# Post-norms that read their scale from PSUM and leave GpSimd out, and bias rows copied from HBM to HBM

## The chip, the cores and the metric

The kernel runs on one core of one Trainium2 chip. Its engines are TensorE (PE in the rows, with PEld for its weight loads), VectorE (DVE), ScalarE (ACT), GpSimd (POOL) and SyncE (SP, which only issues DMAs here). The metric is the device time of one execution in microseconds. Three runs of the kernel before took 3525.71, 3531.94 and 3532.26 us, so the median is 3531.94 us.

## The reference, cut to what matters

A sequence of 512 tokens of width 1024 goes through two hybrid blocks and then through a third block of another kind. All arithmetic is float32. The change touches the third block alone: two of its norms are applied to the output of a branch, before that is added to the residual stream, and its attention has a relative bias table.

```
def rms_norm_2(x, g):
    y = x * rsqrt(mean(x * x, axis=-1, keepdims=True) + 1e-6)
    return y * g

def second_block(x, ...):                     # 512 tokens x 1024
    h = rms_norm_2(x, g_pre_mix)
    z = h @ w_in
    ...                                       # dilated attention (uses rel_bias_table) and a convolution, gated into merged
    x = x + rms_norm_2(merged @ w_mix_out, g_post_mix)
    h = rms_norm_2(x, g_pre_ffn)
    x = x + rms_norm_2(swiglu(h @ w_ffn_in) @ w_ffn_out, g_post_ffn)
    return x

bias = bias_tab[rel_bucket(offset * dilation)]   # 3 groups of 8 heads; a function of query minus key
s = q k / 8 + bias
```

## The kernel before, in words

Activations lie transposed: 8 chunks (`m` or `k`) of 128 channels by 512 tokens. Each product of a weight and an activation is made of three float32r matmuls in `mm3` (L172 high by high, L173 high weight by low activation, L174 low weight by high activation), so every activation needs a high part `h` hi (ScalarE, L239) and a low part lo (VectorE, L240, which needs the high part).

All weights come as one stream of 550 units of 128 x 1024 float32 (512 KB, tensor `wst`). SP issues the load of a unit (L133) into one of 3 staging slots. `w_prep` turns a unit into its high part (ScalarE, L141) and its low part (VectorE, L142) in a ring of 5, up to `LOOK` = 3 units ahead of the one that TensorE uses. One unit holds 8 weight tiles, which is 24 matmuls. The next load into a staging slot is issued only when L142 has read it.

Stages follow one another: `gen_ffn`, `gen_mix` with `gen_side`, `gen_merge` and `gen_ffn` for each of the two layers, then `gen_mix2` with `gen_attn2`, `gen_merge2` and the last `gen_ffn`. The Tile scheduler fixes each engine's order when the program is built, by a simulated timeline and by priorities: `with self.late(-5000)` gives what stands in it an earlier place, and `keep_in_program_order` forbids the scheduler to move an instruction past others so marked. On the chip each engine then runs its list in that order.

`gen_ffn` starts with the columns (0, 1) of gate and up in four PSUM banks, chunk k after chunk k as they arrive, and goes on with column groups 2 to 12. After (0, 1) the statistics of the norm are made: `stats_a` sums the squares over partitions with four matmuls against a column of ones (L218), takes an inverse square root by 12 small VectorE operations (L223, L205 to L210), and `bcast` makes four diagonal blocks (L231) and one matmul with ones (L232) that puts the scale of each token on all partitions of a PSUM bank; ScalarE copies that bank to SBUF (L233).

`bias_rows` is called once, in the first `gen_ffn`, after column group 2. It makes for each of 3 groups a table of 8 heads by 384 positions (L1015, L1018) in 8 partitions of SBUF, and a DMA issued by GpSimd (L1019) writes each row 128 times to `dr_b` in HBM, from where the attention of the third block reads it much later with a shifted pattern.

`post` is the norm after a branch. It is used once over all tokens at the end of `gen_merge2` (the mid post below) and twice, on 256 tokens each, at the end of the last `gen_ffn` (half 0 and half 1). The branch output lies in SBUF, already multiplied by the gain. `post` makes the statistics, copies the scale to SBUF, multiplies each chunk by it (L1351) and adds it to x (L1360). In the mid post `x_done` then makes hi, lo and the squares for the next norm, whose sum GpSimd accumulates (L200). In the two halves some chunks are multiplied and added on GpSimd, and each chunk of x goes out by a DMA on SP (L1362).

Of the kernel before, what the change touches and what calls it, by code (L numbers as in the profile page):

```python
# [9 lines left out]
F32 = mybir.dt.float32  # L10
F32R = mybir.dt.float32r
I32 = mybir.dt.int32
AF = mybir.ActivationFunctionType
ALU = mybir.AluOpType
# [32 lines left out]
A_RB = A_PA + PAR  # L47
A_SM = A_RB + 512
A_X = A_SM + 336
A_Y = A_X + 4096  # L50
# [59 lines left out]
class Build:  # L110
# [113 lines left out]
        self.rsqrt(y, v, a, b)  # L224
        return y

    def bcast(self, cols, dg, ps, out):

        nc = self.nc
        for t in range(cols.shape[-1]):  # L230
            nc.vector.tensor_scalar_mul(dg[:, 128 * t:128 * t + 128], self.f(A_C + C_ID, 128), cols[:, t:t + 1])  # L231
        nc.tensor.matmul(ps, lhsT=self.f(A_C + C_ONE, 128), rhs=dg, start=True, stop=True)  # L232
        nc.scalar.activation(out, ps, AF.Copy)  # L233

    def x_done(self, m, gain):
        hi, lo = self.h(m)
# [7 lines left out]
    def gen_ffn(self, wgu, wdn, l, done, halves=None):  # L244
        nc = self.nc
        Y = A_Y
        gs = [self.f(Y + 1536 + 512 * i, 512) for i in range(2)]
        tt = [self.f(Y + 2560 + 512 * i, 512) for i in range(2)]
        rb = self.f(A_RB, 512)
        ring = tuple(range(8))  # L250

        def fs(c):
            o = R_O + (c % FSLOTS) * 1024
            return self.r(o, 512), self.r(o + 512, 512)

        def gkey(c, up, k):
            return (wgu, l, np.arange(128 * k, 128 * k + 128), np.arange(128) + 128 * c + up * DFF)

        def evac(c, pg, pu):
            i = c % 2  # L260
            nc.vector.tensor_tensor(gs[i], pg, rb, op=ALU.mult)  # L261
            nc.scalar.activation(gs[i], gs[i], AF.Silu)
            nc.vector.tensor_tensor(gs[i], pu, gs[i], op=ALU.mult)  # L263
            hi, lo = fs(c)
            self.split(hi, lo, gs[i])

        def up(cs):
            ps = {(c, up): self.bank(ring) for c in cs for up in (0, 1)}
            order = [(c, up, k) for c in cs for up in (0, 1) for k in range(8)]
            if len(cs) == 2:  # L270
                order.sort(key=lambda e: e[2])
            for c, up, k in order:
                self.mm3(ps[c, up], self.w(gkey(c, up, k)), self.h(k), k == 0, k == 7)
                yield
            if len(cs) == 2:
                pst = self.bank(ring)
                self.bcast(self.stats_a((self.acc,), pst), tt_flat, pst, rb)
            for c in cs:
                evac(c, ps[c, 0], ps[c, 1])
            if cs[0] == 2 and self.first:  # L280
                self.first = False
                self.bias_rows()

        tt_flat = self.f(Y + 2560, 512)

        def down(grp, cs):
            nk = len(cs)
            if grp == 0:
                order = [(m, j) for m in range(8) for j in range(nk)]
            else:  # L290
                order = [(m, j) for m in range(2) for j in range(nk - 1)] + [(m, nk - 1) for m in range(2)]
                order += [(m, j) for m in range(2, 6 if halves else 8) for j in range(nk)]
            ps = {}
            for m, j in order:
                if j == 0:
                    ps[m] = self.bank(ring)
                key = (wdn, l, np.arange(128) + 128 * cs[j], np.arange(128) + 128 * m)
                self.mm3(ps[m], self.w(key), fs(cs[j]), j == 0, j == nk - 1)
                yield
                if j == nk - 1:  # L300
                    done(grp, m, ps[m], tt[m % 2], rb)
            if grp == 0 or not halves:
                return

            tl = {}
            for i in range(2):
                sl = slice(256 * i, 256 * i + 256)
                for m in (6, 7):
                    ps = self.bank(ring)[:, sl]
                    for j in range(nk):  # L310
                        if i == 0:
                            tl[m, j] = self.w((wdn, l, np.arange(128) + 128 * cs[j], np.arange(128) + 128 * m))
                        self.mm3(ps, tl[m, j], [a[:, sl] for a in fs(cs[j])], j == 0, j == nk - 1)
                        yield
                    done(grp, m, ps, tt[m % 2][:, sl], rb, sl)
                halves(i)

        c0 = list(range(11))
        c1 = list(range(11, 22))
        for cs in [(0, 1)] + [(c,) for c in range(2, 13)]:  # L320
            yield from up(cs)
        yield from down(0, c0)
        for c in c1[2:]:
            yield from up((c,))
        yield from down(1, c1)
# [679 lines left out]
    def bias_rows(self):  # L1005

        nc = self.nc
        o = A_Y + 3584
        cb = self.f(o, 2304)[0:32]
        nc.scalar.dma_start(cb, self.ap["cb"])  # L1010
        tab = self.f(o + 2304, 24)[0:32]
        nc.scalar.dma_start(tab, self.ap["par"][2][0:32, 296:320])
        for g in range(3):
            ps = self.bank(tuple(range(8)))
            nc.tensor.matmul(ps[0:8, 0:384], lhsT=tab[:, 8 * g:8 * g + 8], rhs=cb[:, 384 * g:384 * g + 384],  # L1015
                             start=True, stop=True)
            t = self.f(o + 2328 + 384 * g, 384)[0:8]
            nc.vector.tensor_tensor(t, ps[0:8, 0:384], cb[0:8, 1152 + 384 * g:1536 + 384 * g], op=ALU.add)  # L1018
            nc.gpsimd.dma_start(self.dr_b[g], t[:, None, :].to_broadcast([8, 128, 384]))  # L1019

    def gen_mix2(self):
        nc = self.nc
# [312 lines left out]
        o = R_O + 8192 + 1024 * c  # L1335
        return self.r(o, 512), self.r(o + 512, 512)

    def post(self, y, next_gain, rb, ts=range(4), pool=()):

        nc = self.nc  # L1340
        ring = tuple(range(8))
        ps = self.bank(ring)
        sl = slice(128 * ts[0], 128 * ts[-1] + 128)
        c = self.stats_a((self.acc, self.sqt[1]), ps, ts=ts)
        rb = rb[:, sl]
        self.bcast(c, self.f(A_Y + 512, 512)[:, sl], ps[:, sl], rb)
        keep = self.tc.keep_in_program_order
        y = [a[:, sl] for a in y]

        def mul(m):  # L1350
            keep(eng(m).tensor_tensor(y[m], y[m], rb, op=ALU.mult))  # L1351

        def eng(m):
            return nc.gpsimd if m in pool else nc.vector
        mul(0)
        for m in range(8):
            if m < 7:
                mul(m + 1)
            x = self.x(m)[:, sl]
            keep(eng(m).tensor_tensor(x, x, y[m], op=ALU.add))  # L1360
            if next_gain is None:
                nc.sync.dma_start(self.ap["out"][:, m, sl], x)  # L1362
            else:
                self.x_done(m, next_gain)

    def gen_merge2(self, gains):
        nc = self.nc
# [28 lines left out]
        for m, k in order:  # L1396
            if k == 0:
                ps[m] = self.bank(ring)
            self.mm3(ps[m], self.w(("w_mix_out_2", 0, np.arange(128) + 128 * k, np.arange(128) + 128 * m)), self.h(k),
                     k == 0, k == 7)  # L1400
            yield
            if k == 7:
                nc.scalar.activation(y[m], ps[m], AF.Copy)
                self.sq_acc(m, y[m], self.acc, self.sqt, apart=True)
                nc.scalar.activation(y[m], y[m], AF.Copy, scale=gains[:, 56 + m:57 + m])
        self.post(y, gains[:, 64:72], self.f(A_RB, 512))

    def ffn_post(self, gain):
        nc = self.nc
        y = [self.f(A_Y + 3584 + 512 * m, 512) for m in range(8)]  # L1410

        def done(grp, m, ps, t, rb, sl=slice(0, 512)):
            ym = y[m][:, sl]
            nc.vector.tensor_tensor(ym if grp == 0 else t, ps, rb[:, sl], op=ALU.mult)
            if grp == 1:
                nc.vector.tensor_tensor(ym, ym, t, op=ALU.add)
                self.sq_acc(m, ym, self.acc[:, sl], [a[:, sl] for a in self.sqt], apart=True)
                nc.scalar.activation(ym, ym, AF.Copy, scale=gain[:, m:m + 1])

        def half(i):  # L1420
            self.post(y, None, self.f(A_Y + 1536, 512), range(2 * i, 2 * i + 2), ((1, 2, 4, 5, 7), (2, 5))[i])
        return done, half


    def run(self, upto=99, start=0):
        tc, nc, ap = self.tc, self.nc, self.ap
        with tc.tile_pool(name="sb", bufs=1) as sb, tc.tile_pool(name="hp", bufs=1) as self.hp, \
# [9 lines left out]
            self.sqt = [self.f(A_Y + 512 + 512 * i, 512) for i in range(2)]  # L1437
            self.dr_x = dr.tile([128, 4096], F32, name="dr_x")
            self.dr_b = dr.tile([3, 8, 128, 384], F32, name="dr_b")
            self.dr_c = dr.tile([8, 128, 512], F32, name="dr_c")  # L1440
            self.dr_s = dr.tile([512, 12], F32, name="dr_s")
            self.m2 = {}
# [142 lines left out]
```

## Time and profile before

| | |
|---|---|
| median of three runs | 3531.94 us (3525.71 to 3532.26) |
| the profiled execution | 3525.48 us, its span 3523.7 us |
| TensorE busy | 3423.5 us, 97% of the span |
| VectorE, ScalarE, GpSimd busy | 57%, 37%, 9% |
| mean granted clock of TensorE | 0.985 of full speed |
| HBM traffic | 357 MB, 101 GB/s on average |

The span is the time from the first to the last instruction of one profiled execution. Matmuls are pipelined, so their single durations overlap: in steady state TensorE starts 134 of them in 30 us. What is idle on an engine other than TensorE costs nothing by itself.

### The profile page before, as it was taken

What the parts mean: (1) busy time and instruction counts of PE and PEld (TensorE: products, weight loads), DVE (VectorE), ACT (ScalarE), POOL (GpSimd) and SP (SyncE); (2) the same over time, 40 slices, a digit from 0 to 9 for tenths busy, and PEclk for the clock granted to TensorE, in tenths of its full rate; (3) what the DMA queues carried; (4) which work ended last, traced back from release to release, by engine and by line L of the source; (5) the groups of instructions that cost most, each with busy time, mean ns of one, the idle gap of its engine ahead of it and who ended that gap; (6) DMA issues with size and microseconds to landing.
All of it is one profiled execution on the core that took longest, in us unless ns stands there. A gap on an engine that the chain in (4) does not pass through costs nothing.

```text
span 3523.7 us, 43236 instructions
## 1 busy us (share of the span) xinstructions
PE 3423.5 (97%) x16884; PEld 2793.6 (79%) x16884; DVE 1998.7 (57%) x3733; ACT 1316.1 (37%) x2234; POOL 320.0 (9%) x355
## 2 busy tenths in 40 slices
PE   6899999999999999999999999999999999999997
PEld 5688888776888888888887768888877777878886
DVE  4344488566544444344886666443488998554344
ACT  3222354356332233223544464322344443443232
POOL 2000100010300010001000104000111112220002
PEclk8999999999999999999999999999999999999998
DMA  6722322331322222223322314223333224522221
GB/s 149 116 99 96 120 91 87 108 115 54 132 96 96 96 96 96 96 100 116 96 89 98 112 42 149 95 97 100 108 105 92 83 79 141 183 80 98 97 96 54
DMA packets 100814, 357.05 MB, mean 101 GB/s; under 512 B 14168, under 2 KB 16984, under 8 KB 99808
## 3 DMA queue, kind: packets, MB, share of 16 engines
q1 hardware_dynamic: 81504, 290.49, 24.6%
q0 software_dynamic: 18144, 61.76, 6.9%
q8 instruction: 132, 2.16, 0.3%
q10 hardware_dynamic: 960, 2.04, 0.2%
q14 instruction: 74, 0.61, 0.1%
HBM read 320.05 MB, written 32.08 MB: 100 GB/s over the span
## 4 chain that ended last, share of the span: by engine, by line
PE 91%; DMA 3%; DVE 3%; ACT 1%; issue 1%; POOL 0%; DVEq 0%; ACTq 0%; POOLq 0%
PE pb L172 27%; PE pb L173 27%; PE pb L174 27%; DMA af<-wst 2%; PE pb L801 2%; PE pb L793 1%; PE pb L777 1%; PE pb L1193 1%; PE pb L595 1%; PE pb L737 1%; PE pb L1290 1%; PE pb L1266 1%; PE pb L756 0%; DVE af L1351 0%; DVE ar L142 0%
## 5 line engine op out<-in xcount | busy, mean ns | idle before, releaser
L141 ACT ACTIVATE ar<-af 128x1024 fp32r<-128x1024 f32 x550 | 582.7, 1060 | 1517.5 <-PE pb L173 968.2
L172 PE MATMUL pb<-h,ar 128*128 128x512 f32 x2848 | 1114.2, 394 | 33.9 <-ACT ar L141 15.1
L174 PE MATMUL pb<-h,ar 128*128 128x512 f32 x2848 | 1120.1, 393 | 0.1
L173 PE MATMUL pb<-h,ar 128*128 128x512 f32 x2848 | 1119.4, 393 | 0.0
L142 DVE TENSOR_TENSOR ar<-af,ar 128x1024 fp32r<-128x1024 f32 x550 | 687.7, 1251 | 447.6 <-ACT ar L141 446.1
L172 PEld LDWEIGHTS pb<-h,ar 128*128 128x128 f32 x2848 | 538.0, 189 | 151.1 <-ACT h L239 16.2
L174 PEld LDWEIGHTS pb<-h,ar 128*128 128x128 f32 x2848 | 537.7, 189 | 114.6 <-issue 3.2
L173 PEld LDWEIGHTS pb<-h,ar 128*128 128x128 f32 x2848 | 537.9, 189 | 113.6 <-issue 3.2
L173 PE MATMUL pb<-ar 128*128 128x512 f32 (+1 forms) x1254 | 483.2, 386 | 1.2 <-DVE ar L183 1.2
L174 PE MATMUL pb<-ar 128*128 128x512 f32 (+1 forms) x1254 | 482.8, 386 | 0.0
L172 PE MATMUL pb<-ar 128*128 128x512 f32 (+1 forms) x1254 | 481.8, 386 | 0.6 <-DVE af L779 0.5
L172 PEld LDWEIGHTS pb<-ar 128*128 128x128 f32 x1254 | 235.6, 188 | 49.4 <-DVE af L779 1.2
L200 POOL TENSOR_TENSOR af<-af 128x512 f32<-128x512 f32 (+1 forms) x76 | 109.7, 1444 | 1816.5 <-ACT af L198 1805.5
L173 PEld LDWEIGHTS pb<-ar 128*128 128x128 f32 x1254 | 235.6, 188 | 49.0 <-DVE ar L183 2.4
L174 PEld LDWEIGHTS pb<-ar 128*128 128x128 f32 x1254 | 235.6, 188 | 47.1
L263 DVE TENSOR_TENSOR af<-pb,af 128x512 f32<-128x512 f32 x110 | 75.6, 690 | 299.0 <-PE pb L174 297.9
L261 DVE TENSOR_TENSOR af<-pb,af 128x512 f32<-128x512 f32 x110 | 75.5, 691 | 247.0 <-PE pb L174 231.9
L1132 DVE SCALAR_TENSOR_TENSOR af<-af 128x512 f32<-128x512 f32 x240 | 179.4, 748 | 3.6
L172 PE MATMUL pb<-ar,h 128*128 128x256 f32 (+1 forms) x448 | 133.4, 298 | 0.0
L173 PE MATMUL pb<-ar,h 128*128 128x256 f32 (+1 forms) x448 | 132.4, 296 | 0.0
L174 PE MATMUL pb<-ar,h 128*128 128x256 f32 (+1 forms) x448 | 132.0, 295 | 0.0
L180 DVE TENSOR_TENSOR ar<-af,ar 128x512 fp32r<-128x512 f32 (+4 forms) x178 | 114.3, 649 | 16.2 <-ACT ar L179 15.6
(236 smaller groups left out, 3185.3 us busy)
## 6 DMA issues: line engine op xcount, KB each, us to landing
af<-wst SPq DMA_DIRECT2D x550, 512.0 KB, 3.3
dr_g<-af POOLq DMA_DIRECT2D x64, 256.0 KB, 2.3
af<-dr_g POOLq DMA_DIRECT2D x24, 512.0 KB, 4.6
dr_x<-af POOLq DMA_DIRECT2D x3, 2048.0 KB, 7.5
af<-dr_x POOLq DMA_DIRECT2D x3, 2048.0 KB, 8.7
dr_b<-af POOLq DMA_DIRECT2D x3, 1536.0 KB, 63.3
h<-dr_g POOLq DMA_DIRECT2D x16, 256.0 KB, 5.5
af<-x POOLq DMA_DIRECT2D x8, 256.0 KB, 12.3
```

The lines of the kernel that those rows point to most:

```text
L141: self.nc.scalar.activation(self.r(o, UNIT), st, AF.Copy)
L142: self.nc.vector.tensor_tensor(self.r(o + UNIT, UNIT), st, self.r(o, UNIT), op=ALU.subtract)
L172: mm(out, lhsT=w[0], rhs=a[0], start=start, stop=False, skip_group_check=True)
L173: mm(out, lhsT=w[0], rhs=a[1], start=False, stop=False, skip_group_check=True)
L174: mm(out, lhsT=w[1], rhs=a[0], start=False, stop=stop, skip_group_check=True)
L180: self.nc.vector.tensor_tensor(lo, src, hi, op=ALU.subtract)
L200: nc.gpsimd.tensor_tensor(acc, acc, t, op=ALU.add)
L261: nc.vector.tensor_tensor(gs[i], pg, rb, op=ALU.mult)
L263: nc.vector.tensor_tensor(gs[i], pu, gs[i], op=ALU.mult)
L595: self.nc.tensor.transpose(ps[:, 128 * i:128 * i + 128], t[:, 128 * i:128 * i + 128], self.f(A_C + C_ID, 128))
L801: first[u] = self.behind(first[u], mm(out[64 * u:64 * u + 64], lhsT=v[u][:, j, :], rhs=pts[u][:, 128 * j:128 * j + 128], start=first[u] is ...
L1132: nc.vector.scalar_tensor_tensor(a, u[:, j:j + 512], w[:, j:j + 1], a, op0=ALU.mult, op1=ALU.add)
```

## The change

It has four parts. First, `bias_rows` is called after column group 8 instead of 2, and each table row is first written once to a new HBM tensor `dr_r` and from there copied 128 times to `dr_b` by a DMA from HBM to HBM. Second, `post` no longer copies the scale from PSUM to SBUF: VectorE's multiplication reads it from the PSUM bank. Third, `post` uses no GpSimd and no forced order, its statistics get an earlier priority, and in the two halves at the end one operation (and one DMA) takes two chunks of 128 x 256. Fourth, `gen_merge2` squares and scales straight from PSUM instead of from a copy in SBUF.

```
-    def bcast(self, cols, dg, ps, out):
+    def bcast(self, cols, dg, ps, out=None):
...
-        nc.scalar.activation(out, ps, AF.Copy)
+        if out is not None:
+            nc.scalar.activation(out, ps, AF.Copy)
...
-            if cs[0] == 2 and self.first:
+            if cs[0] == 8 and self.first:
                 self.first = False
                 self.bias_rows()
...
-            nc.gpsimd.dma_start(self.dr_b[g], t[:, None, :].to_broadcast([8, 128, 384]))
+            nc.gpsimd.dma_start(self.dr_r[g], t)
+            nc.gpsimd.dma_start(self.dr_b[g], self.dr_r[g][:, None, :].to_broadcast([8, 128, 384]))
...
-    def post(self, y, next_gain, rb, ts=range(4), pool=()):
+    def post(self, y, next_gain, ts=range(4), step=1):
...
-        c = self.stats_a((self.acc, self.sqt[1]), ps, ts=ts)
-        rb = rb[:, sl]
-        self.bcast(c, self.f(A_Y + 512, 512)[:, sl], ps[:, sl], rb)
-        keep = self.tc.keep_in_program_order
-        y = [a[:, sl] for a in y]
-
-        def mul(m):
-            keep(eng(m).tensor_tensor(y[m], y[m], rb, op=ALU.mult))
-
-        def eng(m):
-            return nc.gpsimd if m in pool else nc.vector
+        n = sl.stop - sl.start
+        with self.late(-5000):
+            c = self.stats_a((self.acc, self.sqt[1]), ps, ts=ts)
+            rb = ps[:, sl]
+            self.bcast(c, self.f(A_Y + 512, 512)[:, sl], rb)
+
+        def three(o):
+            return self.f(o, 512 * step).rearrange("p (m t) -> p m t", m=step)[:, :, sl]
+        yv = [three(y + 512 * m) for m in range(0, 8, step)]
+        xv = [three(A_X + 512 * m) for m in range(0, 8, step)]
+        rb = rb[:, None, :].to_broadcast([128, step, n])
+
+        def mul(i):
+            nc.vector.tensor_tensor(yv[i], yv[i], rb, op=ALU.mult)
         mul(0)
-        for m in range(8):
-            if m < 7:
-                mul(m + 1)
-            x = self.x(m)[:, sl]
-            keep(eng(m).tensor_tensor(x, x, y[m], op=ALU.add))
+        for i in range(8 // step):
+            if i + 1 < 8 // step:
+                mul(i + 1)
+            nc.vector.tensor_tensor(xv[i], xv[i], yv[i], op=ALU.add)
             if next_gain is None:
-                nc.sync.dma_start(self.ap["out"][:, m, sl], x)
+                nc.sync.dma_start(self.ap["out"][:, step * i:step * i + step, sl], xv[i])
             else:
-                self.x_done(m, next_gain)
+                self.x_done(i, next_gain)
...
-                nc.scalar.activation(y[m], ps[m], AF.Copy)
-                self.sq_acc(m, y[m], self.acc, self.sqt, apart=True)
-                nc.scalar.activation(y[m], y[m], AF.Copy, scale=gains[:, 56 + m:57 + m])
-        self.post(y, gains[:, 64:72], self.f(A_RB, 512))
+                with self.late(-5000 if m == 7 else 0):
+                    self.sq_acc(m, ps[m], self.acc, self.sqt, apart=True)
+                    nc.scalar.activation(y[m], ps[m], AF.Copy, scale=gains[:, 56 + m:57 + m])
+        self.post(A_Y + 1536, gains[:, 64:72])
...
-            self.post(y, None, self.f(A_Y + 1536, 512), range(2 * i, 2 * i + 2), ((1, 2, 4, 5, 7), (2, 5))[i])
+            self.post(A_Y + 3584, None, range(2 * i, 2 * i + 2), 2)
```

The operations of `ffn_post.done` on a half also get the earlier priority. With the changed file's six added lines, L1351 of before is L1359 there, L1360 is L1364, L240 is L241, L1019 is L1020 and L1021.

On GpSimd at the start of the program, before: the loads of x, the additions of squares for the first norm (L200), and among them the writes of the bias rows.

```order
L1450 DMA af<-x 128x512 x8
L200 ISA
L200 TENSOR_TENSOR af<-af 128x512 x5
L1019 DMA dr_b<-af 1024x1x384
L200 TENSOR_TENSOR af<-af 128x512 x2
L1019 DMA dr_b<-af 1024x1x384 x2
L200 TENSOR_TENSOR af<-af 128x512 x6
```

The same place of the changed kernel:

```order
L1456 DMA af<-x 128x512 x8
L200 ISA
L200 TENSOR_TENSOR af<-af 128x512 x7
L1020 DMA dr_r<-af 8x384 x2
L1021 DMA dr_b<-dr_r 1024x1x384
L1020 DMA dr_r<-af 8x384
L1021 DMA dr_b<-dr_r 1024x1x384 x2
L200 TENSOR_TENSOR af<-af 128x512 x6
```

All seven additions of the first norm now stand ahead of the bias rows, and each copy to `dr_b` has a small write to `dr_r` ahead of it.

On VectorE in the mid post, before: the diagonal blocks of the broadcast, and then multiplication, addition and low part of one chunk after the other.

```order
L231 TENSOR_SCALAR af<-af 128x128 x4
L1351 TENSOR_TENSOR af<-af 128x512 x2
L1360 TENSOR_TENSOR af<-af 128x512
L240 SCALAR_TENSOR_TENSOR h<-af,h 128x512
L1351 TENSOR_TENSOR af<-af 128x512
```

The same place of the changed kernel:

```order
L231 TENSOR_SCALAR af<-af 128x128 x4
L1359 TENSOR_TENSOR af<-af,pb_76 128x512 x8
L1364 TENSOR_TENSOR af<-af 128x512 x8
L241 SCALAR_TENSOR_TENSOR h<-af,h 128x512 x8
L142 TENSOR_TENSOR ar<-af,ar 128x1024 x3
```

The three kinds of operation no longer alternate: eight multiplications, then eight additions, then eight low parts.

On VectorE at the end of the program, before: the last output chunk of half 1 (L1416), VectorE's share of half 0's multiplications and additions, and among them the inverse square root of half 1 (L223, L205 and on).

```order
L1416 TENSOR_TENSOR af<-af 128x256
L1351 TENSOR_TENSOR af<-af 128x256
L1360 TENSOR_TENSOR af<-af 128x256
L1351 TENSOR_TENSOR af<-af 128x256
L223 TENSOR_SCALAR af<-pb_69 128x2
L1360 TENSOR_TENSOR af<-af 128x256
L1351 TENSOR_TENSOR af<-af 128x256
L205 TENSOR_SCALAR af<-af 128x2
L1360 TENSOR_TENSOR af<-af 128x256
L206 TENSOR_SCALAR af<-af 128x2
```

The same place of the changed kernel (L1421 is the last output chunk there):

```order
L1421 TENSOR_TENSOR af<-af 128x256
L1359 TENSOR_TENSOR af<-af,pb_74 128x2x256 x4
L1364 TENSOR_TENSOR af<-af 128x2x256
L223 TENSOR_SCALAR af<-pb_69 128x2
L1364 TENSOR_TENSOR af<-af 128x2x256 x3
L205 TENSOR_SCALAR af<-af 128x2
```

All of half 0 is on VectorE now, and all of it but one small operation stands ahead of half 1's inverse square root. Outside of the first column groups, the mid post and the end, the four engines' lists are the same as before, but for the names of PSUM banks.

## Rows read from the trace of the kernel before

**Rows 1.** Stretches: PE, PEld, DVE, ACT, POOL busy (xcount); PE clock, DMA share, GB/s.

```profile
30.00:60.00 30.00, 13.95 (x66) 11.38 (x64) 3.41 (x7) 3.12 (x3) 0.00 (x0) 0.77 0.57 106
60.00:90.00 30.00, 27.45 (x106) 20.33 (x107) 17.48 (x33) 11.27 (x16) 2.14 (x2) 0.88 0.58 76
90.00:120.00 30.00, 22.80 (x101) 18.56 (x99) 0.69 (x1) 0.00 (x0) 0.00 (x0) 0.97 0.97 69
120.00:150.00 30.00, 22.07 (x72) 16.53 (x73) 12.64 (x16) 10.55 (x14) 0.00 (x0) 0.75 0.86 153
150.00:180.00 30.00, 30.00 (x134) 24.86 (x133) 14.53 (x17) 10.08 (x13) 0.00 (x0) 1.00 0.37 124
```

**Rows 2.** TensorE's waits, 0 to 300 us: total us, times, longest.

```profile
PE pb L232 <- DVE af L231: 18.6, 1, 18.6
PE pb L172 <- ACT ar L141: 15.1, 2, 10.5
PE pb L172 <- ACT h L239: 9.4, 1, 9.4
```

**Rows 3.** ScalarE's waits in the same stretch, for weight loads.

```profile
ACT ar L141 <- DMA af<-wst: 83.2, 9, 34.6
```

**Rows 4.** DMA issues (median us to landing): 20 to 30, 60 to 90, 90 to 120, 0 to 300 us.

```profile
dr_b<-af POOLq DMA_DIRECT2D x1, 1536.0 KB, 35.6
...
dr_b<-af POOLq DMA_DIRECT2D x2, 1536.0 KB, 63.3
...
af<-wst SPq DMA_DIRECT2D x2, 512.0 KB, 48.7
...
af<-wst SPq DMA_DIRECT2D x52, 512.0 KB, 3.3
```

**Rows 5.** Timeline of the mid post: start us, us, instruction [idle before <-releaser].

```profile
3123.73 0.58 ACT L1403 ACTIVATE af<-pb 128x512 f32<-128x512 f32 x1
...
3124.40 0.63 ACT L198 ACTIVATE af<-af 128x512 f32<-128x512 f32 x1
...
3130.25 2.08 PE L232 MATMUL pb<-af 128*128 128x512 f32 x2 [3.41 <-DVE af L231]
...
3132.99 1.29 DVE L1351 TENSOR_TENSOR af<-af 128x512 f32<-128x512 f32 x2 [2.80 <-ACT af L233]
3134.20 0.69 DVE L1360 TENSOR_TENSOR af<-af 128x512 f32<-128x512 f32 x1
3134.93 0.72 ACT L239 ACTIVATE h<-af 128x512 fp32r<-128x512 f32 x1 [1.96 <-DVE af L1360]
...
3135.68 0.75 DVE L240 SCALAR_TENSOR_TENSOR h<-af,h 128x512 fp32r<-128x512 f32 x1 [0.79 <-ACT h L239]
3135.70 2.50 PE L172 MATMUL pb<-h,ar 128*128 128x512 f32 x5 [3.37 <-ACT h L239]
...
3138.00 0.63 PE L173 MATMUL pb<-h,ar 128*128 128x512 f32 x1
...
3138.99 1.33 POOL L200 TENSOR_TENSOR af<-af 128x512 f32<-128x512 f32 x1 [17.96 <-ACT af L198]
3139.09 1.78 DVE L1351 TENSOR_TENSOR af<-af 128x512 f32<-128x512 f32 x1
```

**Rows 6.** A VectorE multiplication with one operand in PSUM: xcount | busy us, mean ns | idle.

```profile
L263 DVE TENSOR_TENSOR af<-pb,af 128x512 f32<-128x512 f32 x110 | 75.6, 690 | 299.0 <-PE pb L174 297.9
```

**Rows 7.** Timeline of the end, from half 1's last output chunk.

```profile
3501.82 0.42 DVE L1416 TENSOR_TENSOR af<-af 128x256 f32<-128x256 f32 x1
...
3506.45 0.68 DVE L205 TENSOR_SCALAR af<-af 128x2 int32<-128x2 int32 x1
...
3511.52 0.16 DVE L210 SCALAR_TENSOR_TENSOR af<-af 128x2 f32<-128x2 f32 x1
...
3512.33 1.22 PE L232 MATMUL pb<-af 128*128 128x256 f32 x2 [8.75 <-DVE af L231]
...
3519.48 0.74 DVE L1360 TENSOR_TENSOR af<-af 128x256 f32<-128x256 f32 x2
```

More of the change, by code (lines that the diff above doesn't have):

```diff
@@ L1413, in done @@
             ym = y[m][:, sl]
[L1414 to L1418, printed above, removed]
+            with self.late(-5000 if sl.stop - sl.start < 512 else 0):
+                nc.vector.tensor_tensor(ym if grp == 0 else t, ps, rb[:, sl], op=ALU.mult)
+                if grp == 1:
+                    nc.vector.tensor_tensor(ym, ym, t, op=ALU.add)
+                    self.sq_acc(m, ym, self.acc[:, sl], [a[:, sl] for a in self.sqt], apart=True)
+                    nc.scalar.activation(ym, ym, AF.Copy, scale=gain[:, m:m + 1])
         def half(i):
-            self.post(y, None, self.f(A_Y + 1536, 512), range(2 * i, 2 * i + 2), ((1, 2, 4, 5, 7), (2, 5))[i])
+            self.post(A_Y + 3584, None, range(2 * i, 2 * i + 2), 2)
         return done, half
@@ L1439, in run @@
             self.dr_b = dr.tile([3, 8, 128, 384], F32, name="dr_b")
+            self.dr_r = dr.tile([3, 8, 384], F32, name="dr_r")
             self.dr_c = dr.tile([8, 128, 512], F32, name="dr_c")
```

## The prediction

> **What bounds the kernel now.** I read the slices of the span first: TensorE is busy nearly everywhere and the chain of work that ended last runs nearly all through it, so a change pays only where TensorE stands still or runs slowly. The slices show that at the start and hardly anywhere else. Cut into stretches of 30 us [rows 1], the steady state is the last row: 134 matmuls in 30 us, 0.224 us each, clock 1.00. From 30 to 150 us, 66 + 106 + 101 + 72 = 345 are started. At 0.224 us they need 77.2 us and they took 120, so 42.8 us are lost there. TensorE's waits [rows 2] give 33.7 of them: 18.6 us of the scale broadcast for VectorE, and 15.1 us for the high part of a weight unit; the third row, 9.4 us, is the start itself and stays. The other 9.1 us are matmuls after each wait at a lower granted clock: 0.77, 0.88 and 0.75 in stretches in which TensorE had stood idle [rows 1], a part of each at the lower of its two levels, 1.2 GHz.
>
> Both waits go back to one cause. ScalarE waited 83.2 us for weight loads [rows 3], and VectorE, which runs its list in order, stood behind it, the inverse square root for the broadcast with it. A weight load lands in 3.3 us in the median, but in 48.7 us between 90 and 120 us, while bias writes are under way [rows 4]: one from about 22 us (35.6 us to land) and two from about 75 us (63.3 us each). The two carry 3.15 MB in 63.3 us, 50 GB/s; the one alone made 1.57 MB in 35.6 us, 44 GB/s. Two at once are no faster together than one, and a weight load reaches 159 GB/s. So the limit is not the number of DMA engines at work but something all three writes share: the eight SBUF partitions that they read, or the HBM that they write.
>
> **Bias rows.** After the change the 128-fold copy reads HBM, and the 8 partitions are read once (12 KB). By the order of GpSimd's list the copies come after the first norm's sums, and by the place of the call after column group 8, near 110 us, when the prepared units are full again. If the source was the limit, the copy runs at up to a weight load's 159 GB/s, 9.9 us each, 30 us for the three. In that time the weights need 512 KB in every 24 x 0.224 = 5.4 us, 97 GB/s. `w_prep` works three units, 16 us, ahead and its load is issued three units before that, so a load may take five times its 3.3 us before anybody waits. Hence the price is 0, and at the other end, if the copies go no faster than the writes do now, the same 42.8 us. I take 1.5 us lost, near the first end, because a limit that does not grow with the DMA engines points at the eight partitions.
>
> The Trainium skill, "SBUF — State Buffer", section "Door 1: The DMA port swizzle", says that a transfer's rate depends on how many of 16 SBUF ports its partitions reach, and by its map partitions 0 to 7 reach two, at about 27 GB/s each. By that rule the writes had a ceiling of 54 GB/s, with which the 44 and 50 GB/s of rows 4 agree, and the HBM source would be free of it. If instead the HBM side sets the 50 GB/s, the first rival below holds.
>
> **The mid post, up to its first matmul.** Rows 5 are the chain. ScalarE squares from PSUM at once instead of after the copy: 3124.40 - 3123.73 = 0.67 us earlier, so the broadcast ends at 3131.66 and not 3132.33. ScalarE's copy of it goes, for which VectorE stood from 3132.33 to 3132.99, 0.66 us; it starts at 3131.7. But its list is now eight multiplications, eight additions, eight low parts. A multiplication from PSUM takes 0.69 us [rows 6], as one from SBUF, and two in a row take 1.29 [rows 5], so 0.62 each behind one another. Eight: 5.0 us, to 3136.7. First addition 0.69, high part 0.72 with the gaps: TensorE starts at about 3138.2, where it started at 3135.70. That is 2.5 us later, although 1.3 us were saved ahead of it.
>
> **The mid post, first low part.** This counts more. After five high-part matmuls TensorE needs the low part, which let it go on at 3138.00. Now this stands behind all eight additions: 8 x 0.62 = 5.0 us, to 3141.7, and 0.75 us of its own, so 3142.5, 4.5 us late. In the meantime GpSimd's sums for the next norm begin, and rows 5 show what that does: a VectorE operation with two SBUF operands took 1.78 us beside L200, against 0.65 in the pair ahead. I add one such hit, 1.1 us. TensorE stands idle twice, and the three waits at the start cost 9.1 us in clock, 3 us each; since it has hardly risen again between the two, I add 0.4. On the other side VectorE was the slower partner for the eight chunks and no longer is, which gives back some 0.5 us of short waits. Sum +5.5 us. From the bounds: 2.5 us late if low parts come as soon as the high parts, 10 us if all eight additions are blocked. After that nothing waits: low parts come every 0.7 to 1.8 us, and TensorE spends 12 x 0.224 = 2.7 us on each chunk.
>
> The Trainium skill, "SBUF — State Buffer", section "Who interferes with whom", says that VectorE with two SBUF inputs and GpSimd reading SBUF block each other for a whole instruction, and one SBUF input does not. The 1.78 us agree. By the rule the multiplications, which now read PSUM, are free, and the additions and low parts, packed into the stretch where GpSimd adds, are not.
>
> **The end.** After the last output chunk (L1416 ends 3502.24) [rows 7] the chain was: half 0's share on VectorE beside GpSimd, the inverse square root from 3506.45 to 3511.68, broadcast to 3513.55, copy, half 1, last addition at 3520.22. Now VectorE alone: four multiplications of 2 x 256 columns, 4 x 0.62 = 2.5 (3504.7); four additions and L223, 2.7 (3507.4); eleven small operations of 0.16 us and a little between them, 2.1 (3509.5; the row of 0.68 stood beside GpSimd); diagonal 3512.33 - 3511.68 = 0.65, broadcast 1.22 (3511.4); four and four operations of half 1, 5.1 (3516.5). 3.7 us earlier; the last DMA has twice the bytes, 0.5 us. Sum -3.2 us, bounds -1 (if the wide PSUM operand costs 0.3 us more each) and -5.5 (if the scheduler had really put half 1's statistics first; its list doesn't: they stand behind half 0).
>
> Earlier squares in the mid post take one ScalarE operation less per chunk, off the path. The three bias matmuls cost the same at their later place.
>
> **Sum.** Against the profiled execution, 3525.5: -42.8 + 1.5 + 5.5 - 3.2 = 3486.5. Two of the three runs shown stand 6.5 us above that execution and the median with them; the trace doesn't say where, so I add 1.5. Forecast 3488 us.
>
> **Rivals.** *The copies are no faster than the writes* (the change does not do what it says): weights starve from about 110 us, as between 75 and 135 us before. 3486.5 + 41.3 = 3528, up to 3534 with the runs' spread. For it: the writes to HBM are the same ones. Against: a limit on the writing side should have let two writes, to different places, run faster than one.
>
> *Half starved*: the copies run at two to three times the old rate, but with their short rows (1.5 KB) delay the weights enough to empty the prepared units once. Half of the 42.8 stays: 3508. For it: weight loads and copies share the same DMA engines. Against: five times a load's normal landing is needed.
>
> *Slower*: the 128 reads of one 1.5 KB row in HBM hold each other up, and the copies run at half of today's rate. The starved stretch then lasts twice as long: 3528 + 42.8 = 3571. It decides from the point where two copies land later than 63 us. Nothing in the trace of before shows an HBM source, so only the bound speaks.
>
> **How the numbers follow.** Forecast 0.72, its own range 3477 to 3500 (mid post 2.5 to 10, end -5.5 to -1, runs' spread 6.5). Half starved 0.13, as fast as before 0.08, slower 0.05, below 3477 0.02. A measurement of this kernel tells about 0.2%, 7 us, from no change. Faster: 0.72 + 0.13 + 0.02 = 0.87, within 0.2%: 0.08, slower: 0.05. The range reaches into the half-starved case: 3477 to 3513.
>
> **What would show it.** Right: TensorE's waits up to 300 us without the 18.6 and 15.1, 134 matmuls in each 30 us from 30 us on, clock 1.00 there; `dr_b` landing in 10 to 30 us; weight loads beside it under 16 us. Mid post: first low-part matmul some 12 us after the broadcast's end, where it was 5.7 (3138.00 - 3132.33). End: last addition about 14 us after the last output chunk, and not 18 (3520.22 - 3502.24). Wrong: `dr_b` landings of 35 us and more, with weight loads behind them.

## The result and the profile after

The changed kernel takes 3486.61 us (median of four runs, 3485.8 to 3489.4), the kernel before beside it 3531.96: a ratio of 0.9877, with an interval of 0.986 to 0.9894. The forecast was 3488 us in a range of 3477 to 3513. The profiled execution took 3486.46 us, 3484.7 of them the span, at a mean granted clock of 0.99. By the medians the change brings 45.4 us. The two profiled executions, from which this section is read, differ by 39.0 us in their spans, since that of the kernel before was 6.5 us faster than its median; where its slower runs lose those 6.5 us, no trace shows.

**The start.** First the stretches, with the columns of [rows 1], then TensorE's waits from 0 to 300 us, which answer to [rows 2], then ScalarE's for weight loads [rows 3], and last the DMA issues from 80 to 200 us [rows 4]:

```profile
30.00:60.00 30.00, 30.00 (x136) 24.61 (x135) 17.69 (x35) 12.86 (x16) 0.00 (x0) 1.00 0.37 123
60.00:90.00 30.00, 30.00 (x134) 24.84 (x133) 11.04 (x13) 8.46 (x11) 0.00 (x0) 1.00 0.31 106
90.00:120.00 30.00, 30.00 (x130) 23.33 (x129) 13.19 (x17) 8.50 (x12) 3.76 (x5) 1.00 0.33 107
120.00:150.00 30.00, 30.00 (x134) 24.84 (x133) 12.62 (x14) 8.54 (x12) 1.11 (x2) 1.00 0.67 233
150.00:180.00 30.00, 30.00 (x134) 24.85 (x133) 11.11 (x13) 7.43 (x8) 0.00 (x0) 1.00 0.27 101
```

```profile
PE pb L172 <- ACT h L240: 9.6, 1, 9.6
```

```profile
ACT ar L141 <- DMA af<-wst: 8.3, 3, 4.4
```

```profile
af<-wst SPq DMA_DIRECT2D x22, 512.0 KB, 3.3
dr_b<-dr_r POOLq DMA_DIRECT2D x3, 1536.0 KB, 13.3
dr_r<-af POOLq DMA_DIRECT2D x3, 12.0 KB, 4.0
```

TensorE is full in all five stretches at clock 1.00, where in the first four it had been busy 13.95 to 27.45 of 30 us at 0.75 to 0.97. Only the wait of the start itself is left. ScalarE waited 83.2 us for weight loads, now 8.3, and the copies take 13.3 us each instead of 35.6 and 63.3. While they run (120 to 150 us) the DMA engines move 233 GB/s, where the old writes together with the weights got 69 [rows 1].

What this is worth is read from a mark behind it that both programs have, GpSimd's first large memset (L461, now L462). It began at 416.25 us and begins now at 374.18. These are the timeline's rows for it and for two later marks, the first L218 of the mid post and the first L218 of half 0. Before:

```profile
416.25 4.28 POOL L461 MEMSET ar<- 128x4992 f32 x1 [2.69 <-PE pb L174]
...
3122.79 0.95 PE L218 MATMUL pb<-af 128*128 128x1 f32 x8
...
3493.32 0.50 PE L218 MATMUL pb<-af 128*128 128x1 f32 x4
```

After (the mid post's L218, at 3081.60, stands in the next timeline):

```profile
374.18 4.28 POOL L462 MEMSET ar<- 128x4992 f32 x1 [2.69 <-PE pb L174]
...
3457.74 0.50 PE L218 MATMUL pb<-af 128*128 128x1 f32 x4
```

The memset comes 42.1 us earlier, while the whole span is 39.0 us shorter (3523.7 - 3484.7), so 3.1 us go back behind it. Between this memset and the mid statistics (the first L218 of the mid post, 3122.79 before and 3081.60 after) the program is the same but for ScalarE's copies in `gen_merge2`, and the stretch is 0.9 us longer. From there to the statistics of half 0 (3493.32 and 3457.74) it takes 376.1 us instead of 370.5, 5.6 more. On to the last output chunk it is 8.9 us in both. From there to the end it takes 18.05 us instead of 21.46, 3.4 less. So -42.1 + 0.9 + 5.6 - 3.4 = -39.0.

**The mid post.** The timeline that answers to [rows 5] (start us, us, instruction, and the idle time before it with what ended it):

```profile
3081.60 0.95 PE L218 MATMUL pb<-af 128*128 128x1 f32 x8
...
3083.16 1.05 PE L218 MATMUL pb<-af 128*128 128x1 f32 x8 [0.62 <-ACT af L198]
...
3087.63 2.08 PE L232 MATMUL pb<-af 128*128 128x512 f32 x2 [3.41 <-DVE af L231]
3089.74 4.87 DVE L1359 TENSOR_TENSOR af<-af,pb 128x512 f32<-128x512 f32 x8 [2.17 <-PE pb L232]
3094.53 7.04 DVE L1364 TENSOR_TENSOR af<-af 128x512 f32<-128x512 f32 x8
3095.25 0.72 ACT L240 ACTIVATE h<-af 128x512 fp32r<-128x512 f32 x1 [11.56 <-DVE af L1364]
3096.02 2.50 PE L172 MATMUL pb<-h,ar 128*128 128x512 f32 x5 [6.32 <-ACT h L240]
...
3097.70 3.32 POOL L200 TENSOR_TENSOR af<-af 128x512 f32<-128x512 f32 x2 [18.10 <-DVE af L1364]
...
3101.50 5.80 DVE L241 SCALAR_TENSOR_TENSOR h<-af,h 128x512 fp32r<-128x512 f32 x4
...
3102.29 0.79 PE L173 MATMUL pb<-h,ar 128*128 128x512 f32 x1 [3.77 <-DVE h L241]
```

The row of eight multiplications, the row of eight additions, and behind them the first low part (L241): TensorE begins 14.42 us after the first L218, and its first low-part matmul (L173) comes after 20.69. Before, these were 12.91 (3135.70) and 15.21 (3138.00). The low part is 5.5 us late, and that is the stretch's loss. The additions take 0.88 us each, the multiplications with the PSUM operand 0.61.

**The end.** The timeline that answers to [rows 7]:

```profile
3466.23 0.42 DVE L1421 TENSOR_TENSOR af<-af 128x256 f32<-128x256 f32 x1
3466.65 2.48 DVE L1359 TENSOR_TENSOR af<-af,pb 128x512 f32<-128x512 f32 x4
3469.05 0.68 DVE L1364 TENSOR_TENSOR af<-af 128x512 f32<-128x512 f32 x1
...
3469.72 1.88 DVE L1364 TENSOR_TENSOR af<-af 128x512 f32<-128x512 f32 x3
3471.53 0.16 DVE L205 TENSOR_SCALAR af<-af 128x2 int32<-128x2 int32 x1
...
3474.30 1.22 PE L232 MATMUL pb<-af 128*128 128x256 f32 x2 [6.53 <-DVE af L231]
3475.55 2.48 DVE L1359 TENSOR_TENSOR af<-af,pb 128x512 f32<-128x512 f32 x4 [1.31 <-PE pb L232]
3477.95 2.49 DVE L1364 TENSOR_TENSOR af<-af 128x512 f32<-128x512 f32 x4
```

The last addition ends 13.8 us after the last output chunk (3480.44 - 3466.65), before 18.0. The operations of the inverse square root take 0.16 us each; beside GpSimd they had taken up to 0.68. From the last addition to the end of the span it is 4.3 us, before 3.5.

### The profile page after: what moved, and what is told of

Same layout as the page of the kernel before. It is cut to its first block, busy times and chain, and to the rows that moved or that the text cites. A ratio compares the mean times of both kernels' runs of the same rounds, so it can differ in the third digit from the quotient of the medians.

```text
span 3484.7 us, 43198 instructions
## 1 busy us (share of the span) xinstructions
PE 3414.7 (98%) x16884; PEld 2789.2 (80%) x16884; DVE 1995.9 (57%) x3731; ACT 1309.2 (38%) x2223; POOL 314.4 (9%) x344
## 4 chain that ended last, share of the span: by engine, by line
PE 93%; issue 3%; DVE 2%; DMA 1%; ACT 1%; POOL 0%; DVEq 0%; POOLq 0%; ACTq 0%
PE pb L172 28%; PE pb L173 28%; PE pb L174 28%; PE pb L802 1%; PE pb L778 1%; PE pb L794 1%; PE pb L1195 1%; PE pb L738 1%; PE pb L1292 1%; PE pb L1268 1%; PE pb L596 0%; PE pb L757 0%; DMA af<-dr_g 0%; PE pb L752 0%; POOL h L985 0%
## 5 line engine op out<-in xcount | busy, mean ns | idle before, releaser
L173 PE MATMUL pb<-h,ar 128*128 128x512 f32 x2848 | 1118.3, 393 | 3.8 <-DVE h L241 3.8
L174 PE MATMUL pb<-h,ar 128*128 128x512 f32 x2848 | 1119.1, 393 | 0.0
L142 DVE TENSOR_TENSOR ar<-af,ar 128x1024 fp32r<-128x1024 f32 x550 | 687.3, 1250 | 384.6 <-ACT ar L141 383.4
L173 PEld LDWEIGHTS pb<-h,ar 128*128 128x128 f32 x2848 | 537.1, 189 | 116.0 <-DVE h L241 4.5
L174 PEld LDWEIGHTS pb<-h,ar 128*128 128x128 f32 x2848 | 537.2, 189 | 112.1 <-issue 2.7
L173 PE MATMUL pb<-ar 128*128 128x512 f32 (+1 forms) x1254 | 483.2, 386 | 1.2 <-DVE ar L183 1.2
L174 PE MATMUL pb<-ar 128*128 128x512 f32 (+1 forms) x1254 | 482.8, 386 | 0.0
L173 PEld LDWEIGHTS pb<-ar 128*128 128x128 f32 x1254 | 235.6, 188 | 48.9 <-DVE ar L183 2.4
L174 PEld LDWEIGHTS pb<-ar 128*128 128x128 f32 x1254 | 235.6, 188 | 47.1
L200 POOL TENSOR_TENSOR af<-af 128x512 f32<-128x512 f32 (+1 forms) x76 | 114.1, 1501 | 1725.9 <-ACT af L198 1706.9
L173 PE MATMUL pb<-ar,h 128*128 128x256 f32 (+1 forms) x448 | 132.4, 296 | 0.0
L174 PE MATMUL pb<-ar,h 128*128 128x256 f32 (+1 forms) x448 | 132.0, 295 | 0.0
## 6 DMA issues: line engine op xcount, KB each, us to landing
dr_b<-dr_r POOLq DMA_DIRECT2D x3, 1536.0 KB, 13.3
af<-x POOLq DMA_DIRECT2D x8, 256.0 KB, 12.9
```

The lines of the kernel that those rows point to most:

```text
L142: self.nc.vector.tensor_tensor(self.r(o + UNIT, UNIT), st, self.r(o, UNIT), op=ALU.subtract)
L173: mm(out, lhsT=w[0], rhs=a[1], start=False, stop=False, skip_group_check=True)
L174: mm(out, lhsT=w[1], rhs=a[0], start=False, stop=stop, skip_group_check=True)
L200: nc.gpsimd.tensor_tensor(acc, acc, t, op=ALU.add)
```

## The experiments

The first four kernels ran on one chip, beside the kernel before with 3528.42 us (seven runs), the last four on another, beside 3529.57 (seven runs). The ratios are to these.

**The place alone.**

```diff
-            if cs[0] == 2 and self.first:
+            if cs[0] == 8 and self.first:
```

> The kernel before with the bias rows only moved from column group 2 to 8; the rows are still written from 8 SBUF partitions. If those partitions are the limit: each write lands in 35 to 90 us, the weight loads beside it in 20 to 50 us, TensorE loses 30 to 55 us between 110 and 220 us, and the time stays at 3515 to 3540 us. Rival, the early place was the trouble (prepared units not yet full, sums of the first norm mixed in): waits of the start gone, 3480 to 3495 us.

Measured: 3509.2 us, ratio 0.9946 (0.9931 to 0.9961). The stretches of this run, then its DMA issues from 80 to 220 us, then what GpSimd's queue moved from 118 to 148 us (packets, MB, share of the 16 engines):

```profile
120.00:150.00 30.00, 30.00 (x134) 24.83 (x133) 6.26 (x7) 3.75 (x6) 0.00 (x0) 1.00 0.98 66
150.00:180.00 30.00, 17.75 (x62) 12.89 (x61) 4.25 (x5) 3.15 (x4) 0.00 (x0) 0.79 0.99 96
180.00:210.00 30.00, 23.28 (x87) 17.91 (x86) 6.12 (x8) 5.80 (x7) 0.00 (x0) 0.87 0.62 116
```

```profile
dr_b<-af POOLq DMA_DIRECT2D x3, 1536.0 KB, 70.5
```

```profile
q0 software_dynamic: 324, 1.49, 94.9%
```

The writes stay as slow as they were: 1.49 MB in 30 us is 50 GB/s for three at once, as for two and nearly as for one. Yet the time falls by 19 us. From 120 to 150 us, with the writes under way, TensorE is still full; it starves only from 150 to 210 us, by (134 - 62) + (134 - 87) = 119 matmuls of 0.224 us, 26.7 us. The memset begins at 401.21, 27.0 us later than with the copies. Before, the one write at the very start alone had cost (134 - 66) x 0.224 = 15.2 us [rows 1]. So the later place alone brings the memset 15 us forward although no transfer gets faster. What differs can be read in the two traces. Before, TensorE stands still from 43.95 us, 22 us after the write was issued, and waits for the norm's broadcast [rows 2]; VectorE's list has the inverse square root for it behind the low parts of two units that came late (L142 at 51.16 and 58.31 us). At the later place no broadcast stands in that list, and TensorE first stands still at 157 us, 44 us after the first write was issued. Whether that broadcast or smaller reserves of prepared units at the start made the difference, no run separates. Neither theory had this: the time lies outside what both expected, and the part of the source is the other 27 us.

**The copy alone**, at the old place after column group 2:

```diff
-            nc.gpsimd.dma_start(self.dr_b[g], t[:, None, :].to_broadcast([8, 128, 384]))
+            nc.gpsimd.dma_start(self.dr_r[g], t)
+            nc.gpsimd.dma_start(self.dr_b[g], self.dr_r[g][:, None, :].to_broadcast([8, 128, 384]))
```

> The kernel before with only the copy from HBM to HBM, at the old place after column group 2. If the 8 partitions are the limit: copies land in 10 to 20 us, the 18.6 and 15.1 us waits of TensorE are gone or under 5 us together, 3480 to 3490 us. Rival, the place decides: at least half of the 42.8 us stays, 3505 us and more.

Measured: 3482.81 us, ratio 0.9872 (0.9856 to 0.9889). The copies land in 14.6 us, TensorE's one wait up to 300 us is the start's 9.2, and the memset begins at 374.12. Its DMA issues from 20 to 100 us:

```profile
dr_b<-dr_r POOLq DMA_DIRECT2D x3, 1536.0 KB, 14.6
```

The copy alone brings all of the 42 us, and the place adds nothing to it.

**Both edits on the bias rows, without the post-norms.** The diffs of the two runs above together.

> The kernel before with both edits of the bias rows and none of the post-norms. My theory: it alone brings 42 us, and the post-norm edits cost 2.2 us on balance (5.6 lost in the mid post, 3.4 won at the end), so this is 2 us faster than the changed kernel in its profiled execution: 3484 us. Rival, the post-norm edits help: 3490 us or more.

Measured: 3484.05 us, ratio 0.9875 (0.986 to 0.9889). That is 2.6 us below the changed kernel, but in another set of runs, and by the ratios to the kernel before the two don't differ (0.9875 and 0.9877). That the post-norms cost 5.6 - 3.4 = 2.2 us rests on the traces alone; the rival's 3490 us or more is excluded. The memset begins at 374.27, and the last output chunk is 21.46 us from the end, as before.

**The source on 128 SBUF partitions, no HBM copy.** Each bias row is made on 16 partitions, and each partition writes it 8 times. The diff is cut to the write itself.

```diff
-            nc.gpsimd.dma_start(self.dr_b[g], t[:, None, :].to_broadcast([8, 128, 384]))
+            nc.gpsimd.dma_start(self.dr_b[g].rearrange("h (j r) c -> (h j) r c", j=16),
+                                t[:, None, :].to_broadcast([128, 8, 384]))
```

> The kernel before, old place, no copy in HBM: the bias matmul makes each row on 16 partitions, so that the 128-fold write reads 128 SBUF partitions, 8 times each; same bytes, same row length, same destination. If the 8 source partitions were the limit: landing of a write 10 to 20 us and 3480 to 3492 us. Rival, the writing side in HBM or the short rows are the limit: 35 to 63 us as before, and 3515 us or more.

Measured: 3485.99 us, ratio 0.988 (0.9866 to 0.9895). The DMA issues from 20 to 240 us:

```profile
dr_b<-af POOLq DMA_DIRECT2D x3, 1536.0 KB, 8.3
```

The same bytes, in the same rows of 1.5 KB, to the same place in HBM: 8.3 us instead of 35.6 to 70.5. So the HBM side and the short rows are cleared, and the source in eight SBUF partitions is what held the writes. The copy from HBM points the same way: it keeps the shape and the 128 reads of each row, and only its source lies elsewhere. Not separated is whether the small number of partitions or the 128 reads of the same row in each set the rate, since this run changes both. The memset begins at 376.20 us, 2 us later than with the copies; where these are lost was not looked into.

**The mid post in turns.** The changed kernel, with `keep` on its multiplications and additions there.

```diff
-            nc.vector.tensor_tensor(yv[i], yv[i], rb, op=ALU.mult)
+            keep(nc.vector.tensor_tensor(yv[i], yv[i], rb, op=ALU.mult))
...
-            nc.vector.tensor_tensor(xv[i], xv[i], yv[i], op=ALU.add)
+            keep(nc.vector.tensor_tensor(xv[i], xv[i], yv[i], op=ALU.add))
```

> The changed kernel, but in the middle post-norm the multiplications and additions are held in turns (mul, mul, add, mul, add, ...) as before the change; the broadcast is still read from PSUM. Theory (the 5.6 us of the middle come from the order alone: eight multiplications, then eight additions, then the low parts): the first matmul after the broadcast comes about 3.6 us earlier than the changed kernel's 6.32 us wait allows, the 3.8 us wait for the low part is gone, and the stretch from the middle statistics to those of half 0 falls from 376.1 to 368 to 371 us; time 3479 to 3482 us. Rival 1 (the loss is the port conflict between VectorE's additions and GpSimd's sums, whatever the order): the stretch stays within 1.5 us of 376.1, time 3485 to 3488. Rival 2 (reading PSUM as the second operand is what is slow): as rival 1, and the multiplications alone take over 1 us each.

Measured: 3477.26 us (3476.61 to 3477.64), ratio 0.9851 (0.9836 to 0.9865), below the changed kernel and below the low end of what was expected. Timeline:

```profile
3079.70 0.95 PE L218 MATMUL pb<-af 128*128 128x1 f32 x8
...
3087.84 1.29 DVE L1359 TENSOR_TENSOR af<-af,pb 128x512 f32<-128x512 f32 x2 [2.17 <-PE pb L232]
3089.05 0.69 DVE L1365 TENSOR_TENSOR af<-af 128x512 f32<-128x512 f32 x1
...
3090.54 2.50 PE L172 MATMUL pb<-h,ar 128*128 128x512 f32 x5 [2.73 <-ACT h L240]
3092.84 0.63 PE L173 MATMUL pb<-h,ar 128*128 128x512 f32 x1
...
3093.82 1.33 POOL L200 TENSOR_TENSOR af<-af 128x512 f32<-128x512 f32 x1 [16.12 <-ACT af L198]
...
3093.93 0.68 DVE L1359 TENSOR_TENSOR af<-af,pb 128x512 f32<-128x512 f32 x1
3094.53 1.18 DVE L1365 TENSOR_TENSOR af<-af 128x512 f32<-128x512 f32 x1
```

The wait for the first high part is 2.73 us instead of 6.32, the wait for the low part is gone, and the stretch takes 368.2 us (3447.90 - 3079.70). That is 7.9 less than in the changed kernel and 2.3 less than before. Both rivals fall: the operands and the sums are the same as in the changed kernel, only the order differs.

**GpSimd's sums left out of the mid post.** The seven sums of squares for the next norm are not made, so that norm's statistics lack them.

```diff
-            if not (apart and m == 7):
+            if not (apart and m == 7 or self.nosum):
```

> The changed kernel without GpSimd's sums of the squares in the middle post-norm's hand-over (seven additions left out, so part of the next norm's statistics is left out). Theory (order is the main loss, the port conflict a small one): the eight additions go from 7.04 to 4.9 to 5.3 us, the first low part comes about 2 us earlier, but the first matmul still waits 6 us for the first high part; the stretch from the middle statistics to half 0's falls by 1.5 to 3 us to 373 to 375, time 3483 to 3485. Rival (the port conflict is the loss): the stretch falls by 5 us or more, to 371 or less, time 3481 or less.

Measured: 3482.24 us, ratio 0.9866 (0.9852 to 0.9881). Timeline (lines are numbered one up here, so L173 is high by high and L174 the low part):

```profile
3079.73 0.95 PE L219 MATMUL pb<-af 128*128 128x1 f32 x8
...
3088.03 4.87 DVE L1360 TENSOR_TENSOR af<-af,pb 128x512 f32<-128x512 f32 x8 [2.17 <-PE pb L233]
3092.82 4.89 DVE L1365 TENSOR_TENSOR af<-af 128x512 f32<-128x512 f32 x8
...
3094.31 2.50 PE L173 MATMUL pb<-h,ar 128*128 128x512 f32 x5 [6.32 <-ACT h L241]
...
3098.44 0.79 PE L174 MATMUL pb<-h,ar 128*128 128x512 f32 x1
```

The additions go from 7.04 to 4.89 us and the stretch to 373.5 (3453.21 - 3079.73), 2.7 less: 2.0 of them by an earlier low part (18.7 us after the first L219 instead of 20.7) and 0.6 behind it. So of the 7.9 us that the order costs against turns, some 2.0 are the additions beside GpSimd's reads, and the larger part is eight operations standing ahead of the one that TensorE needs.

**Statistics of half 1 first.** As the run in turns; at the end half 1's square root and diagonal are placed ahead of half 0's additions (`add()` calls the additions kept back, `self.adds`).

```diff
+            self.bcast(c, self.f(A_Y + 512, 512)[:, sl], rb, keep=ts[0] > 0)
+        if ts[0]:
+            for add in self.adds:
+                add()
```

> As the run with the middle post-norm in turns, and at the end the statistics of half 1 (the eight small matmuls, the root, the two diagonal multiplications) come ahead of half 0's four additions on VectorE. Theory (half 1's broadcast waits for VectorE, which is held by half 0's additions, 1.88 us of them in front): the last addition ends 12 to 13 us after the last output chunk where it was 13.8, and the time is 0.8 to 2 us below that of the run with turns alone. Rival (the root's chain of small operations sets the broadcast's time, and half 0's additions only fill its gaps): the last addition ends within 0.5 us of 13.8 or later, since half 0's additions now stand ahead of half 1's.

Measured: 3477.38 us (3474.28 to 3480.56), ratio 0.9854 (0.9838 to 0.9871). Timeline:

```profile
3455.35 0.42 DVE L1440 TENSOR_TENSOR af<-af 128x256 f32<-128x256 f32 x1
3455.77 2.48 DVE L1364 TENSOR_TENSOR af<-af,pb 128x512 f32<-128x512 f32 x4
...
3461.13 1.22 PE L234 MATMUL pb<-af 128*128 128x256 f32 x2 [4.24 <-DVE af L231]
3465.78 2.49 DVE L1372 TENSOR_TENSOR af<-af 128x512 f32<-128x512 f32 x4
```

In the trace the end is shorter as the theory says: the last addition ends 12.5 us after the last chunk (3468.27 - 3455.77) and not 13.8. The medians do not show it: these four runs spread over 6.3 us, and the median equals that of the run in turns. Whether the edit pays is open; its mechanism is seen, its gain in the time is not.

**Bias rows and end, with the mid post of before.** The changed kernel, in which the mid post calls the old function:

```diff
-        self.post(A_Y + 1536, gains[:, 64:72])
+        self.post_mid(y, gains[:, 64:72], self.f(A_RB, 512))
```

> The changed kernel with the middle post-norm of the kernel before (broadcast copied to SBUF by ScalarE, products in turns, y copied out first), so the bias rows and the end alone are changed. Theory (the terms of the sum add): 3484.05 of the run with the bias rows alone less 3.4 for the end, so 3480 to 3482; the stretch from the middle statistics to half 0's is again 370 to 371.5 us and the end from the last output chunk 18 us. Rival (the end's gain is bought by work pushed ahead of the last chunk): the end's 18 us stay, but the stretch ahead of it is longer by 2 to 3 us, and the time is 3483 to 3485.

Measured: 3481.01 us, ratio 0.9861 (0.9846 to 0.9875); the stretch from the mid statistics is 370.1 us (3453.20 - 3083.06), the end 17.7 us. The terms add, and the rival's longer stretch isn't there.

**The five traces of the mid post together**: us from the first L218 to TensorE's first high-part matmul, to its first low-part matmul, and to the statistics of half 0, and the last two's difference.

| kernel | high part | low part | half 0 | difference |
|---|---|---|---|---|
| before | 12.9 | 15.2 | 370.5 | 355.3 |
| old mid post, new end | 12.5 | 14.8 | 370.1 | 355.4 |
| after | 14.4 | 20.7 | 376.1 | 355.4 |
| after, sums left out | 14.6 | 18.7 | 373.5 | 354.8 |
| after, in turns | 10.8 | 13.1 | 368.2 | 355.1 |

Whatever happens ahead of it, some 355 us follow the first low part, so the moment at which that is ready sets the stretch. These 355 us are not made of the same parts, though. The 5 us from the first low-part matmul, before and after, with the columns of [rows 1]:

```profile
3138.00:3143.00 5.00, 5.00 (x22) 4.09 (x21) 3.78 (x5) 2.16 (x4) 1.45 (x2) 0.91 0.00 0
3102.29:3107.29 5.00, 5.00 (x15) 3.97 (x16) 5.00 (x4) 2.34 (x5) 4.76 (x4) 0.64 0.00 0
```

After its second wait TensorE runs at a granted clock of 0.64 there, against 0.91 before: (0.91 - 0.64) x 5 = 1.35 us more lost. In turn the kernel before lost time later, for the last chunks: 13 matmuls from 3157.48 to 3161.45 us took 3.97 us where 13 x 0.224 are 2.9. In the changed kernel the trace shows no such wait.

## Why the prediction was right

**Bias rows, right in mechanism and size.** Predicted -41.3 us, measured -42.1. The old writes run at 50 GB/s whether two or three are under way, and with the source spread the limit is gone. With this agrees the rule that the prediction weighed, the Trainium skill's "SBUF — State Buffer", section "Door 1: The DMA port swizzle": its some 27 GB/s for a port make an estimated 54 GB/s for the two of partitions 0 to 7. By that map 128 partitions reach all 16 ports, and the row for them here is 8.3 us, 190 GB/s. The allowance of 1.5 us for weights delayed by the copies was not needed.

**The place, wrong where it was priced.** The prediction gave the later place a role (copies "when the prepared units are full again") and its first rival the whole 41.3 us. Neither holds. With fast copies the place is worth nothing measurable (3482.81 and 3484.05 us). With slow writes it is worth 15 to 19, so copies that had stayed slow would have cost 27.0 us and not 41.3. The prediction had added up four starved stretches as if one shortage of a fixed size ran through them. In fact the first write cost its 15.2 us by where it stood, and three writes together at the later place cost about as much as the last two before (119 matmuls there, 28 + 33 + 62 = 123 from 60 to 150 us in [rows 1]).

**The mid post, right in cause and sum, with errors in the steps that cancel.** Predicted +5.5, measured +5.6. The first matmul was to come 2.5 us later and came 1.5 later. The second group of eight small matmuls takes 1.05 us here, the same group in the profile of before took 1.75, and the broadcast ended 0.8 us earlier than worked out. The eight multiplications were put at 5.0 us and took 4.87. The first low part was put at 3143.6 on the old clock, 20.8 us after the first L218; it came at 20.7. The additions were put at 5.0 us and one hit of 1.1, and took 7.04, two such hits; by the run without the sums these 2.15 us are GpSimd's doing. That late low part is the stretch's whole loss (the table above). So the low part came when it was expected because the broadcast was 0.8 us early and GpSimd hit the additions twice and not once; that the two meet within 0.1 us is luck. The two small terms behind it, 0.4 for the clock and -0.5 for shorter waits, were both too small: the rows behind the table give some 1.35 and -1.1 us. That their sum is near nothing, as forecast, is luck as well.

**The end, right in mechanism and size.** Predicted -3.2, measured -3.4: the chain 4.2 us shorter instead of 3.7, and the tail behind the last addition 0.8 us longer instead of 0.5. That the scheduler leaves half 1's statistics behind half 0's additions, as the order shows, is seen in the timeline: L223 at 3469.65 is done early, and L205 follows only at 3471.53, behind three additions.

**The sum.** On the profiled execution 3486.5 was worked out and 3486.46 was taken. That it fits to 0.04 us is luck: the bias rows brought 0.8 us more than worked out, the stretch between the memset and the mid post took 0.9 more, for which the sum had no term, and the smaller misses cancel too. The 1.5 us added for the spread of the runs of before were not needed: the changed kernel's median stands 0.15 us above its profiled execution.

So one edit of the change brings everything at the start, the end's part brings 3.4 us, and the mid post loses 5.6, which turns give back with 2.3 beside. In turns the kernel takes 3477.26 us, the best of the medians.

## What to carry to other kernels

Here a DMA that wrote the same few rows many times was held by the eight partitions that it read from. Where a broadcast write is slow, spread the source, or copy from HBM, before you move the transfer to a quieter place. Where one engine hands chunks over to another, the time of the first complete hand-over (here the low part, not the high part) counts, so operations that are cheaper in a batch still lose if the batch stands ahead of it. And a wait's total is not one shortage: look at each stretch for what was waited for, and for what stood ahead of that in its engine's list.

## What was not expected of the hardware

A broadcast write of 1536 KB from 8 partitions landed after 35.6 us (one), 63.3 (median of two) and 70.5 (median of three), from 128 partitions after 8.3, and as a copy from HBM to HBM after 13.3 to 14.6, beside the weight loads. During GpSimd's sums VectorE's multiplications with one operand in PSUM keep their 0.68 us, while additions with both operands in SBUF, 0.69 alone, take 1.18 to 1.21 and in one case 1.77 (in turns). Before, such a multiplication from SBUF took 1.78 us there [rows 5]. Even the inverse square root's operations on 2 columns went from 0.65 to 0.16 us when GpSimd had nothing to do beside them.
